# Down projection of a two-layer fp32 trunk: seven of sixteen weight pairs by seven products, some low parts of weights formed by a DMA that adds, relu and square of those pairs on ScalarE

## The chip, the core and the metric

The kernel runs on one core of one Trainium2 chip. A core has TensorE (matmuls), VectorE, ScalarE and GpSimd (elementwise work), SyncE (which here only issues DMAs), and 16 DMA engines that move data between HBM and the on-chip memory SBUF. Matmuls write to the banks of PSUM. The metric is the time of the whole kernel on the device, in microseconds (us).

## What is computed

The reference is a decoder trunk of two layers on 256 tokens of width 1024: RMSNorm, attention and a residual, then RMSNorm, an MLP and a residual; a final RMSNorm at the end. The change touches the MLP alone, above all its second matrix, which is 4096 x 1024 in float32:

```python
def squared_relu_mlp(x, w_up, w_down):
    return jnp.square(jax.nn.relu(x @ w_up)) @ w_down
```

## The kernel before

**Two parts for each number.** A float32 matmul is made of three matmuls in the faster format fp32r. Each factor is split in two parts: "hi" is the value rounded to fp32r (ScalarE, a copy, L153), "lo" is the value less hi (VectorE, a subtraction, L154). Then hi x hi, hi x lo and lo x hi are added up in PSUM. `split` (L148) does it for 128 x 1024 weights at a time.

**Weights.** They come from HBM in chunks of 1 MB (`row_chunk`, `col_chunk`, `pair_chunk`) into one of three buffers of the pool `wraw` (tiles "raw"); SyncE issues the load as soon as the buffer's last reader is done. The parts go to the pools `whi` and `wlo`, seven buffers of 128 x 1024 each, which come free in turn as TensorE is done with them. `plan` (L198 to L211) lists all chunks; `chunk(i)` emits the code for two chunks ahead of use. The order of TensorE's instructions is that of the code. On VectorE, ScalarE, GpSimd and SyncE a scheduler lays it out when the program is built, and each engine then works through its list in order.

**Stage of w_up.** 16 chunks of 256 columns; TensorE sums two times 128 columns in PSUM (`up_steps`), and `put_up` (L755) takes them out: ScalarE copies one half (L765), VectorE adds the other (L766), and VectorE forms relu and square in one instruction (L768). Both results are split again into hi and lo for the next stage (L778, L779).

**Stage of w_down.** The 32 row blocks of 128 rows go in 16 pairs of two. `MIXED` (L28) lists 12 pairs, and the kind says how a pair is multiplied. "W" (`whole_pair`, `whole_part`): both blocks, both halves of the 256 tokens and both halves of the 1024 columns, 8 products of 128 x 128 by 128 x 512, each of three matmuls, 24 in all. "S" (`seven_pair`, `seven_part`): the 2 x 2 x 2 blocks are multiplied by the Winograd form of Strassen's scheme, with 7 products and so 21 matmuls. It needs sums of weight blocks, made on VectorE in place in the raw buffer (L184, L185, L188, L189), three splits of 128 x 1024 in place of two (the plain left half, the sums in the right half, and the left half as it was changed in place), one of 128 x 512 (L191, L192), and on the other side sums of the hidden values (L774 to L776, split into `diffs` at L781 and L782). Before, pairs 2, 4, 6, 8 and 10 were S. Row blocks 24 to 31 (`REST`) follow in four chunks of four blocks by 512 columns, and before them `put_products` (L874) adds up what the seven products left in four PSUM banks.

**Pools that matter beside these.** `tmp` (six buffers "t") holds the small tiles of `put_up` and of the S pairs; `act` (two buffers "x2") holds the normed input of w_up, the differences, and later the next layer's inputs or final_norm.

Of the kernel before, what the change touches and what calls it, by code (L numbers as in the profile page):

```python
# [11 lines left out]
ALU = mybir.AluOpType  # L12
# [55 lines left out]
def yoco_kernel(  # L68
# [30 lines left out]
    def f(ap):  # L99
        return ap.bitcast(F32)  # L100
# [98 lines left out]
    for layer in range(2):  # L199
        wq, wk, wv = ([moba_w_qkv[0][:, i * D:(i + 1) * D] for i in range(3)] if layer == 0 else  # L200
                      [fox_w_q[0], w_kv[:, 0:D], w_kv[:, D:2 * D]])
        if layer:
            plan += [(row_chunk, wv, k0, 0) for k0 in (0, CK)]
        for g in range(4):
            plan += [(col_chunk, wq, g * S), (col_chunk, wk, g * S)]
            if g == 1:
                plan += [(row_chunk, wv, k0, NB) for k0 in (0, CK)]
        plan += [(row_chunk, w_o[layer], k0, nb * NB) for nb in range(2) for k0 in (0, CK)]
        plan += [(col_chunk, w_up[layer], i * S) for i in range(FF // S)]
        plan += [({"W": whole_pair, "S": seven_pair}[kind], w_down[layer], p) for kind, p in MIXED]  # L210
        plan += [(row_chunk, w_down[layer], k0, nb * NB) for nb in range(2) for k0 in REST[::CK]]  # L211
    first_of = [0]

    def load(n):
# [431 lines left out]

    fill = []
    for layer in range(2):
        r = inv_rms(sums)
        rbs = []  # L650
        qk = big.tile([P, 2, KC, S], F32, name="b0")
# [96 lines left out]


        hid.clear()  # L750
        both_ = act.tile([P, 2, 16, P], F32R, name="x2")
        diffs = both_[:, 0], both_[:, 1]


        def put_up(fc, accs):  # L755
            if not hid:
                hid.extend([big.tile([P, 16, S], F32R, name=name) for name in names]
                           for names in (("b0", "b1"), ("b2", "b3")))
            hh, hl = hid[0][fc // 16], hid[1][fc // 16]
            n = len(accs)  # L760
            a = slice(fc % 16, fc % 16 + n)
            u = tmp.tile([P, 2, S], F32, name="t")
            for j, ps in enumerate(accs):
                cp = tmp.tile([P, S], F32, name="t")
                nc.scalar.copy(cp, ps[:, S:2 * S])  # L765
                nc.vector.tensor_add(u[:, j], ps[:, 0:S], cp)  # L766
            sq = tmp.tile([P, 2, S], F32, name="t")
            nc.vector.scalar_tensor_tensor(sq[:, 0:n], u[:, 0:n], 0.0, u[:, 0:n], op0=ALU.max, op1=ALU.mult)  # L768
            if fc // 2 in SEVEN:


                us = tmp.tile([P, 3, P], F32, name="t")
                a11, a12, a21 = sq[:, 0, 0:P], sq[:, 1, 0:P], sq[:, 0, P:S]
                nc.vector.tensor_sub(us[:, 0:2], sq[:, 0].rearrange("p (t s) -> p t s", s=P), sq[:, :, P:S])  # L774
                nc.vector.tensor_sub(us[:, 2], us[:, 1], a11)
                nc.vector.tensor_add(a21, us[:, 2], a12)  # L776
                at = slice(3 * SEVEN.index(fc // 2), 3 * SEVEN.index(fc // 2) + 3)
            nc.scalar.copy(hh[:, a], sq[:, 0:n])  # L778
            nc.vector.tensor_sub(hl[:, a], sq[:, 0:n], f(hh[:, a]))  # L779
            if fc // 2 in SEVEN:  # L780
                nc.scalar.copy(diffs[0][:, at], us)  # L781
                nc.vector.tensor_sub(diffs[1][:, at], us, f(diffs[0][:, at]))  # L782

        def up_steps(i, c):
            accs = []
# [73 lines left out]


        def seven_part(c, p, i):
            n = SEVEN.index(p)
            place, at, factor = (
                (prod["w"], hidden_part(2 * p, 0), "b11"), (acc[0, 0], hidden_part(2 * p + 1, 0), "b21"),
                (acc[0, 1], hidden_part(2 * p, 1), "b22"), (prod["u3"], 0, "t3"), (prod["u1"], 1, "t1"),
                (prod["u2"], 2, "t2"), (acc[1, 0], hidden_part(2 * p + 1, 1), "t4"))[i]
            if isinstance(at, int):
                at = diffs[0][:, 3 * n + at], diffs[1][:, 3 * n + at]
            (hi, lo), j = c[factor]
            own = place in prod.values()  # L870
            mm_parts(place, at, (hi[:, j], lo[:, j]), own and n == 0, own and n == len(SEVEN) - 1)


        def put_products():  # L874
# [13 lines left out]
            add(1, 1, z)  # L888

        edge = []  # L890
        for i, (kind, p) in zip(take(len(MIXED)), MIXED):
            if kind == "W":
                fill += [((), 1300, lambda i=i, p=p, j=j: whole_part(chunk(i), p, j), None) for j in range(2)]
            else:
                fill += [((), 650, lambda i=i, p=p, n=n: seven_part(chunk(i), p, n), None) for n in range(7)]
        fill.append(((), 0, put_products, None))
        for nb in range(2 - layer):
            cs = take(len(REST) // CK)

            def rest_part(nb, cs, k, half):  # L900
                mm_rows(acc[half, nb], *hidden(k), half, chunk(cs[(k - REST[0]) // CK]), k % CK, False, k == REST[-1])
                if (k, half) == (REST[-1], 1):
                    down_done(nb, [acc[t, nb] for t in range(2)])

            fill += [((), 648, lambda nb=nb, cs=cs, k=k, half=half: rest_part(nb, cs, k, half),
                      pe.after((("h", nb, 0), 850), (("h", nb, 1), 1500)) if (k, half) == (REST[-1], 1) else None)
                     for k in REST for half in range(2)]
# [5 lines left out]
    cs = take(len(REST) // CK)  # L913
    ps = [acc[half, 1] for half in range(2)]

    def last_chunk(k):
        return chunk(cs[(k - REST[0]) // CK])

    def last_part(half, k, n):
        mm_rows(ps[half], *hidden(k), half, last_chunk(k), k % CK, False, k == n - 1)  # L920


    LAST = 2
# [25 lines left out]
    for k in REST[:-2 * CK]:  # L949
        for half in range(2):  # L950
            last_part(half, k, FF // P)
    for k in range(FF // P - 2 * CK, FF // P):
        last_part(0, k, FF // P)
    add_last(0, ps[0], 0, NB)
    finish(0, mean(square(0, 0, NB), part[:, 0:1]))
    for k in range(FF // P - 2 * CK, FF // P - LAST):
        last_part(1, k, FF // P - LAST)
    add_last(1, ps[1], 0, NB)
    sums_of = part[:, 1:2]
    for n0, (pool, name) in ((0, (psa, "acc")), (S, (psa, "acc"))):  # L960
        p = pool.tile([P, S], F32, name=name)
        for k in range(FF // P - LAST, FF // P):
            xh, xl, kx = hidden(k)
            t = slice(P, 2 * P)
            hi, lo = last_chunk(k)[k % CK // 2]
            for st, mv in ((xh, hi), (xh, lo), (xl, hi)):
                nc.tensor.matmul(p, st[:, kx, t], mv[:, k % 2, n0:n0 + S], start=k == FF // P - LAST and mv is hi and st is xh,
                                 stop=k == FF // P - 1 and st is xl)
# [32 lines left out]
```

## Time and profile before

| | us |
|---|---|
| median of three runs | 592.63 (592.06 to 592.75) |
| profiled execution, its own time | 592.5 |
| its span | 590.8 |
| TensorE busy (matmuls) | 581.8, 98% |
| VectorE busy | 462.7, 78% |
| ScalarE busy | 341.8, 58% |
| GpSimd busy | 10.1, 2% |
| weights read from HBM | 102.32 MB, 175 GB/s over the span |

The stage of w_down of layer 0 begins at 210.07 us of the span. The profile names engines PE (TensorE), PEld (its weight loads), DVE (VectorE), ACT (ScalarE), POOL (GpSimd) and SP (SyncE). A row of a timeline has the start, the length, the engine, the line, the operation and the tiles (out <- in); in brackets stands how long the engine sat idle just before, and whose result ended that. A row with "x5" merges five in succession. SyncE's rows are issues of DMAs, not their duration.

### The profile page before, as it was taken

What the parts mean: (1) busy time and instruction counts of PE and PEld (TensorE: products, weight loads), DVE (VectorE), ACT (ScalarE), POOL (GpSimd) and SP (SyncE); (2) the same over time, 40 slices, a digit from 0 to 9 for tenths busy, and PEclk for the clock granted to TensorE, in tenths of its full rate; (3) what the DMA queues carried; (4) which work ended last, traced back from release to release, by engine and by line L of the source; (5) the groups of instructions that cost most, each with busy time, mean ns of one, the idle gap of its engine ahead of it and who ended that gap; (6) DMA issues with size and microseconds to landing.
All of it is one profiled execution on the core that took longest, in us unless ns stands there. A gap on an engine that the chain in (4) does not pass through costs nothing.

```text
span 590.8 us, 8877 instructions
## 1 busy us (share of the span) xinstructions
PE 581.8 (98%) x3388; PEld 501.0 (85%) x3388; DVE 462.7 (78%) x834; ACT 341.8 (58%) x597; POOL 10.1 (2%) x39
## 2 busy tenths in 40 slices
PE   8999999999999999999999999999999999999995
PEld 6998997788888888888889989978888888888884
DVE  5887476489998878888788976767899896999853
ACT  6766566466566654654674665667565564564622
POOL 3000000000000000000000000000000000000000
PEclk9999999999999999999999999999999999999998
DMA  8984442458566517478446444433766664447601
GB/s 270 315 276 143 143 143 73 143 160 267 161 196 213 164 56 263 161 265 282 156 156 209 146 142 143 141 115 103 205 201 179 200 210 148 174 152 277 216 0 72
DMA packets 70890, 103.94 MB, mean 176 GB/s; under 512 B 1800, under 2 KB 51504, under 8 KB 70848
## 3 DMA queue, kind: packets, MB, share of 16 engines
q1 hardware_dynamic: 70336, 102.26, 53.5%
q0 software_dynamic: 208, 0.59, 0.3%
q8 instruction: 26, 0.43, 0.3%
q10 hardware_dynamic: 304, 0.53, 0.2%
q14 instruction: 16, 0.13, 0.1%
HBM read 102.32 MB, written 1.05 MB: 175 GB/s over the span
## 4 chain that ended last, share of the span: by engine, by line
PE 97%; DMA 1%; SPq 0%; DVE 0%; ACT 0%; issue 0%; POOLq 0%; DVEq 0%; ACTq 0%
PE acc L250 19%; PE acc L254 9%; PE sc L260 5%; PE sc L261 5%; PE sc L262 5%; PE acc L241 5%; PE acc L242 5%; PE acc L243 5%; PE acc L233 5%; PE acc L235 4%; PE acc L234 4%; PE sc L234 2%; PE sc L235 2%; PE sc L233 2%; PE sc L396 2%; PE pv L408 1%
## 5 line engine op out<-in xcount | busy, mean ns | idle before, releaser
L154 DVE TENSOR_TENSOR lo<-raw,hi 128x1024 fp32r<-128x1024 f32 x198 | 238.5, 1220 | 46.4 <-ACT hi L153 45.3
L153 ACT ACTIVATE hi<-raw 128x1024 fp32r<-128x1024 f32 x198 | 205.8, 1058 | 111.2 <-DVE raw L189 35.7
L250 PE MATMUL acc<-x,hi 128*128 128x512 f32 x480 | 164.6, 396 | 0.0
L254 PE MATMUL acc<-x,lo 128*128 128x256 f32 x480 | 124.2, 279 | 0.0
L250 PEld LDWEIGHTS acc<-x,hi 128*128 128x128 f32 x480 | 86.0, 188 | 16.3
L254 PEld LDWEIGHTS acc<-x,lo 128*128 128x128 f32 x480 | 90.5, 188 | 5.3
L241 PE MATMUL acc<-x,hi 128*128 128x256 f32 x256 | 74.1, 289 | 0.0
L242 PE MATMUL acc<-x,hi 128*128 128x256 f32 x256 | 72.4, 283 | 0.0
L243 PE MATMUL acc<-x,lo 128*128 128x256 f32 x256 | 72.4, 283 | 0.0
L765 ACT COPY t<-acc 128x256 f32<-128x256 f32 x60 | 22.3, 372 | 65.8 <-PE acc L250 63.2
L260 PE MATMUL sc<-hi,b 128*128 128x512 f32 x142 | 55.3, 389 | 0.0
L262 PE MATMUL sc<-hi,b 128*128 128x512 f32 x142 | 55.2, 389 | 0.0
L261 PE MATMUL sc<-lo,b 128*128 128x512 f32 x142 | 55.2, 389 | 0.0
L241 PEld LDWEIGHTS acc<-x,hi 128*128 128x128 f32 x256 | 49.0, 191 | 1.8 <-issue 1.7
L242 PEld LDWEIGHTS acc<-x,hi 128*128 128x128 f32 x256 | 49.0, 191 | 0.1
L243 PEld LDWEIGHTS acc<-x,lo 128*128 128x128 f32 x256 | 49.0, 191 | 0.0
L766 DVE TENSOR_TENSOR t<-acc,t 128x256 f32<-128x256 f32 x60 | 25.1, 421 | 14.1 <-ACT t L765 13.0
L381 ACT ACTIVATE t<-t,nm 128x128 f32<-128x128 f32 x64 | 28.3, 443 | 7.6 <-DVE nm L374 7.6
L262 PEld LDWEIGHTS sc<-hi,b 128*128 128x128 f32 x142 | 26.6, 188 | 5.6
L261 PEld LDWEIGHTS sc<-lo,b 128*128 128x128 f32 x142 | 26.7, 188 | 5.5
L260 PEld LDWEIGHTS sc<-hi,b 128*128 128x128 f32 x142 | 26.7, 188 | 5.5
L233 PE MATMUL acc<-hi,b 128*128 128x512 f32 x64 | 26.6, 415 | 0.0
(184 smaller groups left out, 886.8 us busy)
## 6 DMA issues: line engine op xcount, KB each, us to landing
raw<-in_w_up_dram SPq DMA_DIRECT2D x32, 1024.0 KB, 5.7
raw<-in_w_down_dram SPq DMA_DIRECT2D x32, 1024.0 KB, 4.8
raw<-in_moba_w_qkv_dram SPq DMA_DIRECT2D x10, 1024.0 KB, 5.3
raw<-in_w_o_dram SPq DMA_DIRECT2D x8, 1024.0 KB, 4.9
raw<-in_w_kv_dram SPq DMA_DIRECT2D x8, 1024.0 KB, 5.4
raw<-in_fox_w_q_dram SPq DMA_DIRECT2D x4, 1024.0 KB, 5.0
raw<-in_moba_w_qkv_dram SPq DMA_DIRECT2D x3, 512.0 KB, 7.6
h<-in_x_dram SPq DMA_DIRECT2D x2, 256.0 KB
```

The lines of the kernel that those rows point to most:

```text
L153: nc.scalar.activation(hi[:, i:i + n], raw[:, i:i + n], AF.Copy)
L154: nc.vector.tensor_sub(lo[:, i:i + n], raw[:, i:i + n], f(hi[:, i:i + n]))
L233: nc.tensor.matmul(ps, xh[:, kx, t], hi[:, kw % 2], start=start, stop=False)
L234: nc.tensor.matmul(ps, xh[:, kx, t], lo[:, kw % 2], start=False, stop=False)
L241: nc.tensor.matmul(ps, hi[:, k], xh[:, k], start=k == 0, stop=False)
L242: nc.tensor.matmul(ps, hi[:, k], xl[:, k], start=False, stop=False)
L243: nc.tensor.matmul(ps, lo[:, k], xh[:, k], start=False, stop=k == KC - 1)
L250: nc.tensor.matmul(ps, hi[:, k], x2[:, k].rearrange("p t s -> p (t s)"), start=k == 0, stop=k == KC - 1)
L254: nc.tensor.matmul(ps[:, 0:S], lo[:, k], xh[:, k], start=False, stop=False)
L260: nc.tensor.matmul(ps, x[0], w[0], start=start, stop=False)
L261: nc.tensor.matmul(ps, x[0], w[1], start=False, stop=False)
L262: nc.tensor.matmul(ps, x[1], w[0], start=False, stop=stop)
```

## The change

- `MIXED` now has a list for each layer (both are the same): W for pairs 0, 1, 3, 6 and 9, S for pairs 2, 4, 5, 7, 8, 14 and 15. What is left (`REST`) are row blocks 20 to 27.
- `split` takes a `source`. Where it has one, ScalarE writes the negated rounded weights into lo (L156 of the new file) and the rounded ones into hi (L157), and a DMA issued from GpSimd adds the weights from HBM onto lo (L158): lo = w - hi, without VectorE. It is used from pair 3 on: for the second block of each W pair, and for the plain left half of each S pair. That makes nine such DMAs of 512 KB in a layer.
- `put_up` forms relu and square of S pairs in two steps on ScalarE (L793, L794) in place of one on VectorE.
- The differences of the first five S pairs are split as before; those of pairs 14 and 15 go to a second tile "x2", in the buffer that held w_up's input.

```diff
+BY_DMA = (1,)
+FIRST = 2
+MIXED = [[("W", 0), ("W", 1), ("S", 2), ("W", 3), ("S", 4), ("S", 5), ("W", 6), ("S", 7), ("S", 8), ("W", 9), ("S", 14), ("S", 15)],
...
-    def split(raw, pieces=1):
+    def split(raw, pieces=1, source=None):
         hi = whi.tile([P] + list(raw.shape[1:]), F32R, name="hi")
         lo = wlo.tile([P] + list(raw.shape[1:]), F32R, name="lo")
+        if source is not None:
+            nc.scalar.activation(lo, raw, AF.Copy, scale=-1.0)
+            nc.scalar.activation(hi, raw, AF.Copy)
+            nc.gpsimd.dma_start(lo, source, accum_op=ALU.add)
+            return hi, lo
...
     def whole_pair(w, p):
         raw = pair_chunk(w, p)
-        return [split(raw[:, k].rearrange("p (n c) -> p n c", c=NB)) for k in range(2)]
+        rows = [w[(2 * p + k) * P:(2 * p + k + 1) * P].rearrange("p (n c) -> p n c", c=NB) for k in range(2)]
+        return [split(raw[:, k].rearrange("p (n c) -> p n c", c=NB), source=rows[k] if k in BY_DMA and p > FIRST else None)
+                for k in range(2)]
...
-        plain = split(left)
+        plain = split(left, source=w[2 * p * P:(2 * p + 2) * P, 0:NB].rearrange("(c p) n -> p c n", p=P) if p > FIRST else None)
...
+        def split_diffs():
+            while len(diffs) < len(kept):
+                n = len(diffs)
+                if n % 5 == 0:
+                    room.append(act.tile([P, 2, 16, P], F32R, name="x2"))
+                dh, dl = (room[-1][:, i, n % 5 * 3:n % 5 * 3 + 3] for i in range(2))
+                nc.scalar.copy(dh, kept[n])
+                nc.vector.tensor_sub(dl, kept[n], f(dh))
+                diffs.append((dh, dl))
...
-            nc.vector.scalar_tensor_tensor(sq[:, 0:n], u[:, 0:n], 0.0, u[:, 0:n], op0=ALU.max, op1=ALU.mult)
-            if fc // 2 in SEVEN:
+            if fc // 2 in seven:
+                nc.scalar.activation(u[:, 0:n], u[:, 0:n], AF.Relu)
+                nc.scalar.activation(sq[:, 0:n], u[:, 0:n], AF.Square)
+            else:
+                nc.vector.scalar_tensor_tensor(sq[:, 0:n], u[:, 0:n], 0.0, u[:, 0:n], op0=ALU.max, op1=ALU.mult)
```

**The lists of the engines.** In the new file `split` has its lines at L162 (hi) and L163 (lo), and the additions of an S pair are L195, L196, L199 and L200 (L184, L185, L188 and L189 before), its 128 x 512 split L202 and L203. The numbers behind tile names tell buffers of one name apart. The first place is ScalarE's list early in the stage of w_down of layer 0. Before, from the changed left half of S2 on (raw_2389 is pair 2, raw_2436 pair 3, raw_2470 pair 4), it reads:

```order
L153 ACTIVATE hi_2408<-raw_2389 128x1024
L153 ACTIVATE hi_2438<-raw_2436 128x1024
L153 ACTIVATE hi_2442<-raw_2436 128x1024
L153 ACTIVATE hi_2475<-raw_2470 128x1024
L153 ACTIVATE hi_2483<-raw_2470 128x1024
L153 ACTIVATE hi_2489<-raw_2470 128x1024
```

In the new program the same stretch (raw_2409 is pair 2, raw_2456 pair 3, raw_2491 pair 4, raw_2536 pair 5) reads:

```order
L162 ACTIVATE hi_2428<-raw_2409 128x1024
L162 ACTIVATE hi_2458<-raw_2456 128x1024
L157 ACTIVATE hi_2462<-raw_2456 128x1024
L157 ACTIVATE hi_2496<-raw_2491 128x1024
L162 ACTIVATE hi_2505<-raw_2491 128x1024
L156 ACTIVATE lo_2463<-raw_2456 128x1024
L156 ACTIVATE lo_2497<-raw_2491 128x1024
L202 ACTIVATE t_2546<-t_2538 128x512
L162 ACTIVATE hi_2511<-raw_2491 128x1024
L157 ACTIVATE hi_2541<-raw_2536 128x1024
```

The negated copies of pair 3 (lo_2463) and pair 4 (lo_2497), on which the adding DMAs wait, stand sixth and seventh, behind the rounded copies.

The second place is VectorE's list where the last S pairs begin. Before (raw_2626 is pair 8, raw_2670 pair 9, raw_2704 pair 10) it reads:

```order
L184 TENSOR_TENSOR t_2706<-raw_2704 128x512
L154 TENSOR_TENSOR lo_2646<-raw_2626,hi_2645 128x1024
L185 TENSOR_TENSOR raw_2704<-raw_2704 128x512
L154 TENSOR_TENSOR lo_2673<-raw_2670,hi_2672 128x1024
L154 TENSOR_TENSOR lo_2677<-raw_2670,hi_2676 128x1024
L192 TENSOR_TENSOR t_2714<-t_2706,t_2713 128x512
L154 TENSOR_TENSOR lo_2710<-raw_2704,hi_2709 128x1024
```

In the new program (raw_2661 is pair 8, raw_2741 pair 14, raw_2786 pair 15) it reads:

```order
L163 TENSOR_TENSOR lo_2682<-raw_2661,hi_2681 128x1024
L195 TENSOR_TENSOR t_2743<-raw_2741 128x512
L163 TENSOR_TENSOR lo_2712<-raw_2709,hi_2711 128x1024
L196 TENSOR_TENSOR raw_2741<-raw_2741 128x512
L203 TENSOR_TENSOR t_2752<-t_2743,t_2751 128x512
L195 TENSOR_TENSOR t_2788<-raw_2786 128x512
L199 TENSOR_TENSOR raw_2741<-raw_2741 128x512
L196 TENSOR_TENSOR raw_2786<-raw_2786 128x512
L163 TENSOR_TENSOR lo_2756<-raw_2741,hi_2755 128x1024
L200 TENSOR_TENSOR raw_2741<-raw_2741 128x512
```

Pair 15 takes the raw buffer of pair 8, which lo_2682 is the last to read, and its first instruction (t_2788) now stands ahead of the rest of pair 14.

The third place is ScalarE's list just after that, where L200 above has to be done before hi_2761:

```order
L162 ACTIVATE hi_2761<-raw_2741 128x1024
L157 ACTIVATE hi_2791<-raw_2786 128x1024
L162 ACTIVATE hi_2800<-raw_2786 128x1024
L156 ACTIVATE lo_2792<-raw_2786 128x1024
L162 ACTIVATE hi_2806<-raw_2786 128x1024
```

There is no such row before: lo_2710, the plain low part of the last S pair, was VectorE's (above), and now lo_2792, the negated copy, is fourth here, with its DMA behind it.

## Rows read from the trace of the kernel before

**Rows 1.** The page's first part: busy us (share) x instructions of each engine.

```profile
PE 581.8 (98%) x3388; PEld 501.0 (85%) x3388; DVE 462.7 (78%) x834; ACT 341.8 (58%) x597; POOL 10.1 (2%) x39
```

**Rows 2.** The page's fourth part: the chain that ended last, by engine.

```profile
PE 97%; DMA 1%; SPq 0%; DVE 0%; ACT 0%; issue 0%; POOLq 0%; DVEq 0%; ACTq 0%
```

**Rows 3.** Windows: length; busy PE, PEld, DVE, ACT, POOL; clock, DMA share, GB/s.

```profile
215.00:235.00 20.00, 20.00 (x90) 16.56 (x89) 17.59 (x21) 10.98 (x12) 0.00 (x0) 1.00 0.49 171
235.00:255.00 20.00, 20.00 (x90) 16.54 (x89) 17.59 (x21) 10.98 (x12) 0.00 (x0) 1.00 0.55 204
```

**Rows 4.** Timeline of TensorE: first matmul of w_down, first of the remaining chunks.

```profile
210.07 0.40 PE L260 MATMUL sc<-hi,b 128*128 128x512 f32 x1
...
271.97 0.39 PE L233 MATMUL sc<-hi,b 128*128 128x512 f32 x1
```

**Rows 5.** The chain that ended last in order of time: two chunks of w_up.

```profile
198.81 0.47 PE acc L250 x2
204.41 0.47 PE acc L250 x2
```

**Rows 6.** Timeline of VectorE: end of w_up and start of w_down.

```profile
185.48 0.42 DVE L766 TENSOR_TENSOR t<-acc,t 128x256 f32<-128x256 f32 x1
185.83 0.28 DVE L775 TENSOR_TENSOR t<-t 128x128 f32<-128x128 f32 x1
186.14 0.29 DVE L776 TENSOR_TENSOR t<-t 128x128 f32<-128x128 f32 x1
186.45 1.22 DVE L154 TENSOR_TENSOR lo<-raw,hi 128x1024 fp32r<-128x1024 f32 x1
187.59 0.55 DVE L782 TENSOR_TENSOR x<-t,x 128x384 fp32r<-128x384 f32 x1
188.06 0.68 DVE L779 TENSOR_TENSOR b<-t,b 128x512 fp32r<-128x512 f32 x1
188.66 0.42 DVE L766 TENSOR_TENSOR t<-acc,t 128x256 f32<-128x256 f32 x1
...
210.73 0.42 DVE L766 TENSOR_TENSOR t<-acc,t 128x256 f32<-128x256 f32 x1 [2.37 <-ACT t L765]
...
217.27 0.68 DVE L189 TENSOR_TENSOR raw<-raw 128x512 f32<-128x512 f32 x1
...
219.09 5.77 DVE L154 TENSOR_TENSOR lo<-raw,hi 128x1024 fp32r<-128x1024 f32 x5 [0.53 <-ACT hi L153]
```

**Rows 7.** Timeline of ScalarE in the same stretch.

```profile
212.58 0.63 ACT L191 ACTIVATE t<-t 128x512 fp32r<-128x512 f32 x1
...
217.99 4.86 ACT L153 ACTIVATE hi<-raw 128x1024 fp32r<-128x1024 f32 x5 [2.31 <-DVE raw L189]
```

**Rows 8.** Timeline of SyncE: issues of w_down's loads.

```profile
222.61 0.37 SPq L172 DMA_DIRECT2D raw<-in_w_down_dram  x1
229.89 3.24 SPq L172 DMA_DIRECT2D raw<-in_w_down_dram  x2
240.17 2.64 SPq L172 DMA_DIRECT2D raw<-in_w_down_dram  x2
```

**Rows 9.** Timeline of VectorE: S pairs that wait for a load; a last pair's splits.

```profile
228.03 0.69 DVE L184 TENSOR_TENSOR t<-raw 128x512 f32<-128x512 f32 x1 [1.85 <-DMA raw<-in_w_down_dram]
237.59 0.69 DVE L184 TENSOR_TENSOR t<-raw 128x512 f32<-128x512 f32 x1 [0.65 <-DMA raw<-in_w_down_dram]
248.27 0.69 DVE L184 TENSOR_TENSOR t<-raw 128x512 f32<-128x512 f32 x1 [1.66 <-DMA raw<-in_w_down_dram]
253.49 2.35 DVE L154 TENSOR_TENSOR lo<-raw,hi 128x1024 fp32r<-128x1024 f32 x2
```

**Rows 10.** The page's sixth part: DMA issues, KB each, median us to landing.

```profile
raw<-in_w_down_dram SPq DMA_DIRECT2D x32, 1024.0 KB, 4.8
x<-in_final_norm_dram POOLq DMA_DIRECT2D x1, 512.0 KB, 4.0
```

**Rows 11.** GpSimd's instruction for that load; ns min/median/max, start.

```profile
L826 POOL DMA_DIRECT2D x<-in_final_norm_dram x1: 588/588/588, 500.8 to 500.8; - x1
```

More of the change, by code (lines that the diff above doesn't have):

```diff
@@ L209, in yoco_kernel @@
         plan += [(col_chunk, w_up[layer], i * S) for i in range(FF // S)]
-        plan += [({"W": whole_pair, "S": seven_pair}[kind], w_down[layer], p) for kind, p in MIXED]
-        plan += [(row_chunk, w_down[layer], k0, nb * NB) for nb in range(2) for k0 in REST[::CK]]
+        plan += [({"W": whole_pair, "S": seven_pair}[kind], w_down[layer], p) for kind, p in MIXED[layer]]
+        plan += [(row_chunk, w_down[layer], k0, nb * NB) for nb in range(2) for k0 in REST[layer][::CK]]
     first_of = [0]
@@ L648, in yoco_kernel @@
     for layer in range(2):
+        mixed, seven, rest = MIXED[layer], SEVEN[layer], REST[layer]
         r = inv_rms(sums)
@@ L750, in yoco_kernel @@
         hid.clear()
[L751 to L752 removed]
+        diffs, kept = [], []
+        def split_diffs():
[7 more added lines that the diff above has]
+                diffs.append((dh, dl))
+        room = []
         def put_up(fc, accs):
@@ L776, in put_up @@
                 nc.vector.tensor_add(a21, us[:, 2], a12)
-                at = slice(3 * SEVEN.index(fc // 2), 3 * SEVEN.index(fc // 2) + 3)
             nc.scalar.copy(hh[:, a], sq[:, 0:n])
             nc.vector.tensor_sub(hl[:, a], sq[:, 0:n], f(hh[:, a]))
-            if fc // 2 in SEVEN:
-                nc.scalar.copy(diffs[0][:, at], us)
-                nc.vector.tensor_sub(diffs[1][:, at], us, f(diffs[0][:, at]))
+            if fc // 2 in seven:
+                kept.append(us)
+                if len(kept) <= 5 or fc + 2 == FF // P:
+                    split_diffs()
         def up_steps(i, c):
@@ L861, in seven_part @@
         def seven_part(c, p, i):
-            n = SEVEN.index(p)
+            n = seven.index(p)
             place, at, factor = (
@@ L867, in seven_part @@
             if isinstance(at, int):
-                at = diffs[0][:, 3 * n + at], diffs[1][:, 3 * n + at]
+                at = tuple(d[:, at] for d in diffs[n])
             (hi, lo), j = c[factor]
             own = place in prod.values()
-            mm_parts(place, at, (hi[:, j], lo[:, j]), own and n == 0, own and n == len(SEVEN) - 1)
+            mm_parts(place, at, (hi[:, j], lo[:, j]), own and n == 0, own and n == len(seven) - 1)
         def put_products():
@@ L890, in yoco_kernel @@
         edge = []
-        for i, (kind, p) in zip(take(len(MIXED)), MIXED):
+        for i, (kind, p) in zip(take(len(mixed)), mixed):
             if kind == "W":
@@ L897, in yoco_kernel @@
         for nb in range(2 - layer):
-            cs = take(len(REST) // CK)
+            cs = take(len(rest) // CK)
             def rest_part(nb, cs, k, half):
-                mm_rows(acc[half, nb], *hidden(k), half, chunk(cs[(k - REST[0]) // CK]), k % CK, False, k == REST[-1])
-                if (k, half) == (REST[-1], 1):
+                mm_rows(acc[half, nb], *hidden(k), half, chunk(cs[rest.index(k) // CK]), k % CK, False, k == rest[-1])
+                if (k, half) == (rest[-1], 1):
                     down_done(nb, [acc[t, nb] for t in range(2)])
             fill += [((), 648, lambda nb=nb, cs=cs, k=k, half=half: rest_part(nb, cs, k, half),
-                      pe.after((("h", nb, 0), 850), (("h", nb, 1), 1500)) if (k, half) == (REST[-1], 1) else None)
-                     for k in REST for half in range(2)]
+                      pe.after((("h", nb, 0), 850), (("h", nb, 1), 1500)) if (k, half) == (rest[-1], 1) else None)
+                     for k in rest for half in range(2)]
             pe.run([edge, fill], fill)
@@ L910, in yoco_kernel, with last_part @@
                 edge += norm_steps(nb, [(gs[:, 2], *xkv[:2]), (gs[:, 1], *xa[:2])])
-    cs = take(len(REST) // CK)
+    cs = take(len(rest) // CK)
     ps = [acc[half, 1] for half in range(2)]
     def last_chunk(k):
-        return chunk(cs[(k - REST[0]) // CK])
-    def last_part(half, k, n):
-        mm_rows(ps[half], *hidden(k), half, last_chunk(k), k % CK, False, k == n - 1)
+        return chunk(cs[rest.index(k) // CK])
+    def last_part(half, k, last):
+        mm_rows(ps[half], *hidden(k), half, last_chunk(k), k % CK, False, k == last)
     LAST = 2
@@ L947, in finish @@
         nc.scalar.dma_start(outr[:, half, NB:D], y[:, NB:D])
-    for k in REST[:-2 * CK]:
+    for k in rest[:-2 * CK]:
         for half in range(2):
-            last_part(half, k, FF // P)
-    for k in range(FF // P - 2 * CK, FF // P):
-        last_part(0, k, FF // P)
+            last_part(half, k, rest[-1])
+    for k in rest[-2 * CK:]:
+        last_part(0, k, rest[-1])
     add_last(0, ps[0], 0, NB)
     finish(0, mean(square(0, 0, NB), part[:, 0:1]))
-    for k in range(FF // P - 2 * CK, FF // P - LAST):
-        last_part(1, k, FF // P - LAST)
+    for k in rest[-2 * CK:-LAST]:
+        last_part(1, k, rest[-1 - LAST])
     add_last(1, ps[1], 0, NB)
@@ L961, in yoco_kernel @@
         p = pool.tile([P, S], F32, name=name)
-        for k in range(FF // P - LAST, FF // P):
+        for k in rest[-LAST:]:
             xh, xl, kx = hidden(k)
@@ L966, in yoco_kernel @@
             for st, mv in ((xh, hi), (xh, lo), (xl, hi)):
-                nc.tensor.matmul(p, st[:, kx, t], mv[:, k % 2, n0:n0 + S], start=k == FF // P - LAST and mv is hi and st is xh,
-                                 stop=k == FF // P - 1 and st is xl)
+                nc.tensor.matmul(p, st[:, kx, t], mv[:, k % 2, n0:n0 + S], start=k == rest[-LAST] and mv is hi and st is xh,
+                                 stop=k == rest[-1] and st is xl)
         add_last(1, p, n0, n0 + S)
```

7 lines of the change are left out of this document (4 added, 3 removed).

## The prediction

> **What bounds the kernel now.** I read the page's first part, then the chain that ended last, then the stage of w_down itself. TensorE is busy 581.8 of 590.8 us [rows 1], and the chain that ended last is TensorE for 97% of the span [rows 2]. Within the stage of w_down it is busy for every microsecond of both windows, at full clock, while VectorE has 17.59 of 20 us and ScalarE 10.98 of 20 [rows 3]. So a matmul taken out is time won, as long as nobody makes TensorE wait for weights, and VectorE has little left to give. From the first matmul of the stage at 210.07 us to the first of the remaining chunks at 271.97 lie 273 matmuls, seven whole pairs of 24 and five pairs of seven products with 21 [rows 4]. That is 61.90 / 273 = 0.2267 us each: 5.44 us for a whole pair (W below), 4.76 for a pair by seven products (S below). Times below are counted from the first of these matmuls, t = 0 at 210.07; S8 is pair 8 by seven products, and its "more" is the third split, that of the left half after it was changed in place.
>
> **What is removed.** Two more pairs of each layer go from 24 matmuls to 21: 4 x 3 = 12 matmuls, 12 x 0.2267 = 2.72 us, 1.36 a layer, all on the bounding engine. If nothing waits, the time is 592.5 - 2.7 = 589.8 us. Everything else in the change lies on engines beside TensorE, and the question is whether the weights still come in time.
>
> **What is moved to other engines.** VectorE has 7 splits fewer a layer in this stage (nine go to the DMAs, two more S pairs bring two) and ten additions more: 10 x 0.69 - 7 x 1.22 = -1.6 us, and about as much again in the up stage. ScalarE gains eleven activations of 128x1024 and sixteen of 128x512 a layer: 11 x 1.06 + 16 x 0.62 = 21.6 us (durations below). It has the room by share. In the up stage these fit: a chunk takes TensorE 5.6 us [rows 5], and two splits with the work of one S pair stay under that on both engines, so I price the up stage at nothing; cover gone, it would show as TensorE waiting for a PSUM bank at L789. The shares hide what matters: in the stage of w_down each engine works its list in order, and the weights run through three raw buffers. So I add up one chain.
>
> **Pitches for the chain.** On VectorE one instruction follows the other after 1.14 us for 128x1024 (186.45 to 187.59), 0.60 for 128x512 (188.06 to 188.66), 0.47 for 128x384, 0.35 for 128x256 and 0.31 for 128x128; the last of a row is done 1.22 us after its start for 128x1024 and 0.69 for 128x512 [rows 6]. On ScalarE five copies of 128x1024 take 4.86 us, so 0.95 pitch and 1.06 for the last; 128x512 takes 0.62 [rows 7]. From engine to engine I count 0.05 (217.95 to 217.99) [rows 6, 7]. A raw buffer is asked for again by SyncE when its last split ends, and VectorE goes on with the new data after 228.03 - 222.61 = 5.42, 237.59 - 232.76 = 4.83 and 248.27 - 242.44 = 5.83 us (the second of two issues starts at the row's start plus its length less 0.37) [rows 8, 9]. I call this reload R and take 5.4, the mean of the three.
>
> **The chain, step by step.** Start: the last up column reaches VectorE at 0.66 [rows 6]. In the order after, that pair (15) is an S pair, so VectorE waits for relu and square on ScalarE, 1.1 + 2 x 0.62 = 2.35, and then has thirteen instructions up to L200 of S2 (lines of the new file): seven of 128x512 (4.2), one of 128x1024 (1.14), one of 384 (0.47), one of 256 (0.35), two of 128 (0.62), then L200 itself from 9.2 to 9.9. The copy "hi" of S2's more (ScalarE) ends at 11.0, its low part (VectorE) at 12.25. In the kernel before the same low part ended at 219.09 + 1.22 - 210.07 = 10.24 [rows 6].
> (1) This frees the raw buffer for S5. Its data come at 12.25 + R; VectorE does L195, L199, L196, L200 (1.8 + 0.69), ScalarE the copy (1.06), VectorE the low part (1.22): 4.9 us, and S4's buffer is free.
> (2) That buffer takes S7. After R, L195 and the last low part of S5: 1.8 us.
> (3) S5's buffer takes S8. After R, five of 128x512, three of 128x1024 and L200 on VectorE (6.4 + 0.69), then copy and low part of S8's more: 9.5 us.
> (4) S8's buffer takes S15. After R, L195, L199, L196, one split and L200 (3.6), then on ScalarE three copies and at last the negated copy of S15's plain part (3 x 0.95 + 1.06): 7.6 us.
> (5) Only now can the adding DMA of S15 start; it needs L us.
> TensorE wants this low part with the second matmul of S15, after 246 + 1 matmuls: 247 x 0.2267 = 56.0. So it comes late by 12.25 + 4.9 + 1.8 + 9.5 + 7.6 + 4R + L - 56.0 = 4R + L - 20 us. In the kernel before, the low part of the last S pair was done at 253.49 + 1.22 - 210.07 = 44.6 [rows 9], and TensorE wanted it after 229 matmuls, at 51.9: 7.3 us early. Two S pairs in a row, twice, and a DMA at the chain's end use that up and more.
>
> **What the adding DMA costs (L).** No DMA that adds is in the trace. From below: a plain DMA of the same 512 KB from GpSimd's queue took 4.0 us to land [rows 10]. From above: twice that, 8.0, if what lies in the buffer is fetched in a pass of its own. I take 5.0, since it has to read 512 KB of weights and 512 KB of the buffer, and a 1024 KB load takes 4.8 [rows 10]; it is nearest to that row. GpSimd's own 0.59 us for the issue [rows 11] is a part of it.
> The Trainium skill ("DMA: Bandwidth & Descriptors", section "Anatomy of one DMA") gives about 2.0 us plus bytes / 436e3 for a DMA from GpSimd: 3.2 us for 512 KB, an estimate by that page, under the 4.0 of the row, and it says nothing of adding. By it the delay would be 4.8 us a layer and the time 599.4.
>
> **The sum.** With R = 5.4 and L = 5.0 the delay is 21.6 + 5.0 - 20 = 6.6 us a layer. It falls in four pieces, whose total is the 6.6: the low part of W3's second half is the sixth copy after S2's more on ScalarE (9.95 + 5 x 0.95 + 1.06 = 15.75), lands at 20.75 and is wanted at 82 x 0.2267 = 18.6: 2.1 us. S5, S8 and S15 wait for theirs by the same working, some 1, 0.5 and 3 us. Less the 1.36 won: 5.24 a layer, and the second layer's lists stand in the same order, so 10.5 us in all. The profiled execution takes 592.5 us (span 590.8 and 1.7 around it), 0.1 under the median 592.63: 592.5 + 10.5 = 603.0 us. The layer-1 load of final_norm now stands in GpSimd's queue ahead of S15's adding DMA; it waits for S8's products (before 50 with the delays so far), so it costs its issue at most, 0.6 us, hidden by S15's wait for ScalarE.
>
> **Ends.** Low: R = 4.8 (the shortest of the three), L = 4.0: 3.2 us late, 592.5 + 2 x (3.2 - 1.36) = 596.2. High: R = 6.8 (the longest, 5.83, and once more the 1.0 by which a load beside another is longer than one alone) and L = 8.0: 15.2 late, 592.5 + 2 x 13.8 = 620.
>
> **Rivals.** (a) The DMA engines become the bound. Nine adding DMAs in some 42 us bring 4.7 MB of weights and as much of the buffer: 225 GB/s on top of some 190. The stretches show 171 GB/s at a share of 0.49 and 204 at 0.55 [rows 3], so full engines give about 350 to 370. Loads and adds would then wait for each other, R and L both at their high ends or over: about 620 us. For it: the sum over the limit. Against it: whether the buffer's own bytes count so is not seen here. The Trainium skill (same page, "Issuing engines are not separate DMA queues") says that DMAs of all queues run on the same 16 engines; the 5.83 beside 4.83 agrees. (b) It works as drawn: no wait, 589.8. The place is the negated copy and adding DMA of S15; it is decided at 4R + L under 20, for R = 4.8 at L under 0.8. Against it: the plain DMA's 4.0. For it: the chain holds 36 us of my pitches, and 5% less of these is 1.8 us. (c) The waits just eat the gain, 4R + L about 21.4: R = 4.8 and L = 2.2, 592.5 us. (d) The change doesn't shed VectorE's work as it says, since ScalarE's list then holds it up at L199 (which waits for both copies of the plain part): that is within the chain and would lengthen steps 3 and 4, towards the high end.
>
> **How the numbers follow.** Forecast (one chain of reloads, 596 to 615) 0.71; (a) with the long end of (d) 0.18; (c) 0.05; (b) 0.06. Predicted: 603.0 us. The range 595.5 to 620 leaves out (b), (c) and about half of (a). Faster by over 0.2% (under 591.4): 0.06; within 0.2%, about what can be told from no change: 0.05; slower: 0.89.
>
> **What would show it.** TensorE no longer busy throughout the stage: waits at L271 to L273 for a DMA into "lo", four a layer, the longest at S15, 5 to 8 us a layer. From the stage's first matmul to the first of the remaining chunks 267 x 0.2267 = 60.5 us plus the delay, so 66 to 69 in place of 61.9. Landing times of the adding DMA give L, those of w_down's loads R (the forecast is wrong if L is under 3 or R under 4.8). ScalarE's busy time some 40 us higher, VectorE's a few lower, the up stage as long as before. If the waits are there but at the loads into "raw" and the DMA share is near 1, it was (a); if TensorE doesn't wait, the chain is wrong.

## The result, and the profile after

The changed kernel takes 620.0 us (median of four runs, 616.8 to 621.6) against 592.5 us: a ratio of 1.0452, with an interval of 1.0431 to 1.0474. It is 27.5 us slower; the forecast was 10.5 us slower, and 620 was the far end of its range. The profiled execution of the changed kernel took 618.5 us, with a span of 616.8.

The page's first part (busy us, share, instructions) and its fourth (the chain that ended last, by engine) answer to [rows 1, 2]:

```profile
PE 587.5 (95%) x3376; PEld 502.0 (81%) x3376; DVE 457.6 (74%) x842; ACT 383.1 (62%) x655; POOL 29.7 (5%) x57
```

```profile
PE 74%; DMA 12%; DVE 8%; ACT 3%; issue 2%; SPq 0%; POOLq 0%; DVEq 0%; ACTq 0%
```

TensorE has 12 matmuls fewer, as drawn, but the chain that was 97% TensorE is now 12% DMA and 8% VectorE. The issues on the page's sixth part answer to [rows 10] (KB each, median us to landing):

```profile
raw<-in_w_down_dram SPq DMA_DIRECT2D x32, 1024.0 KB, 6.1
lo<-in_w_down_dram POOLq DMA_DIRECT2D x18, 512.0 KB, 8.9
```

The loads of w_down took 4.8 us before. The same two stretches of the w_down stage as [rows 3], in windows (length; busy PE, PEld, DVE, ACT, POOL; clock, DMA share, GB/s):

```profile
215.00:235.00 20.00, 14.81 (x63) 11.94 (x62) 15.33 (x20) 12.68 (x16) 3.35 (x3) 0.90 0.60 154
235.00:255.00 20.00, 18.87 (x76) 14.79 (x74) 12.02 (x15) 12.35 (x14) 3.25 (x3) 0.93 0.93 256
```

TensorE, without a gap before, makes 63 and 76 matmuls where it made 90; the DMA share goes from 0.55 to 0.93 in the second stretch, and even VectorE is less busy. The time is lost in this stage alone: from its first matmul (209.7 us) to the first of the remaining chunks (285.0) it takes 75.3 us in the first layer and 74.9 in the second, against 61.9 before [rows 4], in either layer. That is 13.4 and 13.0 us more, 26.5 together, and the span grew by 26.0.

The chain that ended last in the first layer's stage, in order of time (start us, us, what):

```profile
220.42 1.24 DVE lo L163
221.68 4.81 DMA raw<-in_w_down_dram
226.50 0.69 DVE t L195
...
230.19 1.24 DVE lo L163
231.44 7.96 DMA raw<-in_w_down_dram
239.42 0.69 DVE t L195
240.11 1.15 DVE lo L163
241.28 5.78 DMA raw<-in_w_down_dram
...
255.49 1.24 DVE lo L163
256.74 9.93 DMA raw<-in_w_down_dram
...
273.45 0.96 ACT lo L156
274.40 0.29 issue
274.69 5.58 DMA lo<-in_w_down_dram
280.32 0.50 PE acc L272
```

This is the chain of the prediction, link by link: four reloads into raw buffers, the negated copy of S15 on ScalarE, its adding DMA, and TensorE's second matmul of S15. TensorE starts it at 280.32, t = 70.6, where it wanted 56.0: 14.6 us late.

### The profile page after: what moved, and what is told of

Read it like the earlier page. It is cut to its first block, busy times and chain, and to the rows that moved or that the text cites. A ratio compares the mean times of both kernels' runs of the same rounds, so it can differ in the third digit from the quotient of the medians.

```text
span 616.8 us, 9006 instructions
## 1 busy us (share of the span) xinstructions
PE 587.5 (95%) x3376; PEld 502.0 (81%) x3376; DVE 457.6 (74%) x842; ACT 383.1 (62%) x655; POOL 29.7 (5%) x57
## 4 chain that ended last, share of the span: by engine, by line
PE 74%; DMA 12%; DVE 8%; ACT 3%; issue 2%; SPq 0%; POOLq 0%; DVEq 0%; ACTq 0%
PE acc L261 18%; PE acc L265 9%; DMA raw<-in_w_down_dram 9%; PE acc L252 5%; PE acc L254 5%; PE acc L253 5%; PE acc L244 4%; PE acc L246 4%; PE acc L245 4%; DVE lo L163 3%; PE sc L246 2%; PE sc L244 2%; PE sc L245 2%; DMA lo<-in_w_down_dram 2%; PE sc L407 2%
## 5 line engine op out<-in xcount | busy, mean ns | idle before, releaser
L163 DVE TENSOR_TENSOR lo<-raw,hi 128x1024 fp32r<-128x1024 f32 x184 | 223.2, 1221 | 57.7 <-ACT hi L162 55.9
L162 ACT ACTIVATE hi<-raw 128x1024 fp32r<-128x1024 f32 x184 | 192.2, 1058 | 92.8 <-PE acc L253 27.8
L272 PE MATMUL sc<-lo,b 128*128 128x512 f32 x122 | 50.3, 412 | 10.9 <-DMA lo<-in_w_down_dram 10.8
L273 PE MATMUL sc<-hi,b 128*128 128x512 f32 x122 | 49.5, 406 | 0.0
L271 PE MATMUL sc<-hi,b 128*128 128x512 f32 x122 | 49.3, 404 | 0.0
L272 PEld LDWEIGHTS sc<-lo,b 128*128 128x128 f32 x122 | 24.1, 198 | 17.7 <-DMA lo<-in_w_down_dram 12.6
L158 POOL DMA_DIRECT2D lo<-in_w_down_dram x18 | 19.6, 1090 | 276.6 <-ACT lo L156 158.4
L195 DVE TENSOR_TENSOR t<-raw 128x512 f32<-128x512 f32 x14 | 9.7, 690 | 27.1 <-DMA raw<-in_w_down_dram 24.9
L273 PEld LDWEIGHTS sc<-hi,b 128*128 128x128 f32 x122 | 24.3, 199 | 5.1
```

The lines of the kernel that those rows point to most:

```text
L271: nc.tensor.matmul(ps, x[0], w[0], start=start, stop=False)
L272: nc.tensor.matmul(ps, x[0], w[1], start=False, stop=False)
L273: nc.tensor.matmul(ps, x[1], w[0], start=False, stop=stop)
```

## The experiments

Each edit is to the changed kernel. Ratios are to the kernel before, run on the same chip.

### No adding DMA, and the old order with it

Two suspects go with the seven pairs: the adding DMAs, and pairs by seven products that stand in a row. One run has the new order without the DMAs, one the old order (five such pairs, each between whole pairs) with nine adding DMAs a layer.

```
-BY_DMA = (1,)
-FIRST = 2
+BY_DMA = ()
+FIRST = 99
```

> The changed kernel with its seven pairs, relu and square on ScalarE, but no adding DMA: VectorE forms every low part, the nine 512 KB adds of a layer are gone. Theory (loads of w_down queue behind the adds, so the chain of four reloads is 7.1 us a piece in place of 5.4, and the last add is on top): reloads land in about 5 us again, TensorE waits 0 to 4 us a layer for VectorE alone, 590 to 598 us, nearest 595. Rival (S pairs in a row are too much for VectorE and ScalarE, DMA or not, and nine splits more make it worse): 605 us or over.

Measured 596.5 us, ratio 1.0069 (1.0053 to 1.0085): the main theory. Of the distance of 30.2 us between 620.0 and the 589.8 of the count, 23.5 go with the adding DMAs (less what VectorE's nine splits more cost) and 6.7 are left without them. The trace shows some 4 us of these as waits of TensorE for ScalarE and VectorE; how they divide between the new order and VectorE's longer list is not shown.

```
-... ("S", 4), ("S", 5), ("W", 6), ("S", 7), ("S", 8), ("W", 9), ("S", 14), ("S", 15)
+... ("S", 4), ("W", 5), ("S", 6), ("W", 7), ("S", 8), ("W", 9), ("S", 10), ("W", 11)
```

> The five S pairs of the kernel before, in its order (every S pair between two W pairs), with the nine adding DMAs a layer and relu and square on ScalarE. Theory: the adds alone make loads and low parts late; reloads land in 6 us or more, the 7 us of slack at the last S pair are used up, 597 to 606 us, nearest 601. Rival (the pairs in a row cause it): no waits of TensorE, 592 to 593 us.

Measured 604.3 us, 1.0203 (1.0187 to 1.0218). The adds cost 11.8 us even where no two such pairs are neighbours; the rival is out. TensorE waits 2.5 us for the add of W3's second half and 0.6 for that of S4's plain left half. The second one, issued 0.9 us behind the first, is the late link in the chain of the first layer:

```profile
223.94 12.12 DMA lo<-in_w_down_dram
```

### What of the add it is: the bytes, or the adding

The same DMA as a plain copy, and an add that covers one eighth of its columns:

```
-            nc.gpsimd.dma_start(lo, source, accum_op=ALU.add)
+            nc.gpsimd.dma_start(lo, source)
```

> The changed kernel with the nine DMAs of a layer as plain copies in place of adds: same issue, same 512 KB from HBM, same place in the lists, but the buffer's own bytes are not read (the low parts are then wrong, so the output is not the reference's). If reading the buffer and adding costs the DMA engines a pass of its own: landing 4 to 6 us in place of 8.9, loads nearer to 5.4, delay about 9 us a layer, 604 to 611 us. Rival (the adds cost what any 512 KB cost): 618 to 622 us.

Measured 601.3 us, 1.0149 (1.0128 to 1.0171), under the expected band and far from the rival.

```
-            nc.gpsimd.dma_start(lo, source, accum_op=ALU.add)
+            nc.gpsimd.dma_start(lo[:, 0:1, 0:P], source[:, 0:1, 0:P], accum_op=ALU.add)
```

> The changed kernel with each adding DMA cut to an eighth (128 of 1024 columns a partition, 64 KB; the rest of the low part stays unfinished, so the output is not the reference's). The wait for an add and its fixed time stay, its traffic is nearly gone. Theory (traffic): reloads 5.4 us, landing 3 to 4.5, delay 4R + L - 20 = 5 to 6 us a layer, 599 to 603 us. Rival (an add is slow whatever its size): landing 6 us and over, 606 us and over.

Measured 597.7 us, 1.0092 (1.0075 to 1.0109), a little under the expected band: the path over ScalarE, GpSimd's queue and a DMA costs about 1 us beside no add at all, as long as few bytes go over it. That is net of the splits that VectorE is spared: TensorE still waits 2.2 us in the first layer and 2.1 in the second for W3's low part.

So bytes matter, and adding them matters more. The page's third part has the time of the queues (packets, MB, share of the 16 engines' span); the row of GpSimd's queue for the changed kernel, for the plain copy and without those DMAs, one fence each:

```profile
q0 software_dynamic: 4336, 10.03, 8.5%
```

```profile
q0 software_dynamic: 4336, 10.03, 4.9%
```

```profile
q0 software_dynamic: 208, 0.59, 0.3%
```

The same packets and bytes take (8.5 - 0.3)% of 616.8 us = 50.6 us of all engines as adds and (4.9 - 0.3)% of 601.3 = 27.7 us as copies: 2.8 and 1.5 us for one of 512 KB, 1.83 times as much. With copies the first layer's four reloads were 4.75, 4.78, 4.80 and 5.50 us, at or under the R of the prediction; with adds they were 4.81, 7.96, 5.78 and 9.93. In the second layer the copies give back only a part: 4.71, 4.82, 7.44 and 6.04, against 4.81, 7.75, 5.67 and 7.99.

### A fourth raw buffer

If the chain of reload after reload sets the time, a fourth raw buffer must give it back. Room comes from the buffers of the parts, so that a control is needed:

```
-    whi = ctx.enter_context(tc.tile_pool(name="whi", bufs=7))
-    wlo = ctx.enter_context(tc.tile_pool(name="wlo", bufs=7))
+    whi = ctx.enter_context(tc.tile_pool(name="whi", bufs=6))
+    wlo = ctx.enter_context(tc.tile_pool(name="wlo", bufs=6))
```

> The changed kernel with six instead of seven buffers each for the high and the low parts; a control for the next one. Theory: the chain of reloads goes through the three raw buffers and not through these, so 617 to 624 us, nearest 620. Rival (the low parts' buffers are a link of the chain, since a negated copy needs a free one before its add can start): 626 us or more.

Measured 615.0 us, 1.0390 (1.0376 to 1.0403): 5 us less than the changed kernel, and less than expected. Why fewer buffers help is not settled; its chain has reloads of 4.90, 7.37, 5.47 and 6.89 us and a last add of 8.15, 32.8 us in place of 34.1.

```
-    wraw = ctx.enter_context(tc.tile_pool(name="wraw", bufs=3))
+    wraw = ctx.enter_context(tc.tile_pool(name="wraw", bufs=4))
```

> The same six buffers of each, and a fourth raw buffer in the room that comes free, so that each reload may start one pair earlier. Theory (the lateness of 14.6 us a layer is a chain of reload after reload, each waiting for the last work on its buffer): most of it goes; what stays is the engines' own time, about 25 us of adds and 52 us of loads a layer against some 65 us with what is loaded ahead, so 4 to 6 us late a layer: 598 to 609 us, nearest 604. Rival (the DMA engines are full and set the time whatever the buffers): within 1% of the control, 614 us or more.

Measured 615.1 us, 1.0381 (1.0368 to 1.0395): no change against the control. The theory of the chain of buffers fell. VectorE hardly waits for loads any more (6.4 us in all at L195, against 24.9 in the changed kernel), and the wait has moved into the adds, which now take 10.1 us at the median:

```profile
raw<-in_w_down_dram SPq DMA_DIRECT2D x32, 1024.0 KB, 5.1
lo<-in_w_down_dram POOLq DMA_DIRECT2D x18, 512.0 KB, 10.1
```

With the fourth buffer kept, the add becomes a copy:

> Four raw buffers and six of each part, as in the run before with those, but the DMA of the low part copies in place of adding (the same bytes on the same queue from the same places; these low parts are then wrong). Theory (with four raw buffers it is the DMA engines that are full: 25 us of adds beside 52 us of loads a layer; as copies they take 14 us): 594 to 602 us, nearest 598, at least 13 us under the same kernel with adds. Rival (the time lies in the path from the load over ScalarE, GpSimd and the second DMA to TensorE, whatever the engines' share): 608 us or more.

Measured 600.7 us, 1.0138 (1.0114 to 1.0163), 14.4 us under the same kernel with adds: the theory of full engines. One window over most of the first layer's stage (columns as above), for four raw buffers with adds, four with copies, the changed kernel, no adds, and the kernel before:

```profile
228.00:288.00 60.00, 51.15 (x211) 40.57 (x210) 41.00 (x49) 37.41 (x39) 8.54 (x8) 0.94 0.98 273
```

```profile
228.00:288.00 60.00, 56.52 (x252) 46.48 (x252) 48.69 (x56) 41.73 (x46) 4.78 (x8) 1.00 0.89 305
```

```profile
228.00:288.00 60.00, 48.69 (x201) 38.49 (x200) 39.23 (x47) 35.76 (x39) 7.67 (x7) 0.94 0.94 259
```

```profile
228.00:288.00 60.00, 57.03 (x250) 46.09 (x249) 55.37 (x65) 34.67 (x40) 0.00 (x0) 1.00 0.60 212
```

```profile
228.00:288.00 60.00, 60.00 (x270) 49.80 (x269) 50.44 (x57) 33.31 (x43) 0.00 (x0) 1.00 0.65 228
```

With four buffers and adds the DMA engines are busy 0.98 of these 60 us, move 273 GB/s, and TensorE makes 211 matmuls. With copies they move 305 GB/s at 0.89, and it makes 252. So engines that are full set the time; with three raw buffers it shows in the chain of reloads, with four in the adds. Much of it then goes with a single add. The first layer's stage with four buffers and adds is 12.6 us longer than the 60.5 of the count. TensorE waits 8.9 us in it for low parts, 5.5 of them for W3's second half, and comes back from that wait at half its clock (below) for a dozen matmuls:

```profile
234.56 0.80 PE L272 MATMUL sc<-lo,b 128*128 128x512 f32 x1 [5.50 <-DMA lo<-in_w_down_dram]
```

### Fewer adds

Seven adds a layer (without W3's and S4's), then two (only the second blocks of W6 and W9):

```
-FIRST = 2
+FIRST = 4
```

> The changed kernel without the two first adding DMAs of a layer (whole pair 3 and seven-product pair 4 on VectorE): seven adds a layer from pair 5 on. Theory (the DMA engines are full from the first add to the last, so each add taken away gives back its 2.8 us of the engines, less VectorE's 1.2 us for the low part): 620 less 4 x 2.8 to 4 x 1.6, 608.7 to 613.6 us, nearest 611. Rival one (the chain of reloads with unchanged waits for its other links: only the second load gets 2.5 us shorter and VectorE longer by as much): 616 us or more. Rival two (the first wait of TensorE and its half clock cost time of their own, 5.2 us and more a layer): 607 us or less.

Measured 606.4 us, 1.0234 (1.0217 to 1.0251), under the band of the theory and within that of rival two. The four adds gave back 13.6 us. Both things that I had set against each other are seen: in the first layer the reloads for S7 and S8 are back at 4.79 and 4.75 us, and TensorE's first long wait with its half clock (below) is gone. In the second layer a later wait, of 2.7 us, still ends at half clock. How much is whose, this run doesn't tell.

```
-FIRST = 2
+FIRST = 3
-        plain = split(left, source=w[...] if p > FIRST else None)
+        plain = split(left, source=None)
```

> The changed kernel with two adding DMAs a layer instead of nine (second block of pairs 6 and 9 only); the other seven low parts on VectorE. By the count 589.8 us if nothing waits. Theory (an add takes 50.6 / 18 = 2.8 us of all DMA engines, and these only stretch the stage where they are full, which two adds do not do; what stays is VectorE, relieved of 2 x 1.23 us a layer against 596.5 us without any add): 592 to 596 us, nearest 594, and the w_down load back at 4.7 to 5.0 us. Rival (each add costs its share of the 23.5 us between no add and eighteen, 1.3 us): 596.5 + 4 x 1.3 = 601.7 us, 599 us or more.

Measured 604.3 us, 1.0207 (1.0192 to 1.0222): the theory missed, since two adds are worse than none by 7.8 us, and the rival has the number but not the reason. It is one add a layer, that of W6. TensorE's timeline there, and GpSimd's (start us, us, instruction, in brackets the idle time before it and what ended that):

```profile
243.39 0.39 PE L271 MATMUL sc<-hi,b 128*128 128x512 f32 x1
248.19 0.79 PE L272 MATMUL sc<-lo,b 128*128 128x512 f32 x1 [4.42 <-DMA lo<-in_w_down_dram]
248.78 0.63 PE L273 MATMUL sc<-hi,b 128*128 128x512 f32 x1
249.21 0.63 PE L271 MATMUL sc<-hi,b 128*128 128x512 f32 x1
```

```profile
240.20 0.91 POOL L158 DMA_DIRECT2D lo<-in_w_down_dram  x1 [114.25 <-ACT lo L156]
```

TensorE wanted the low part at 243.8. Without adds TensorE does not wait there, so VectorE has it in time; here ScalarE has its negated copy ready at 240.2, 3.6 us ahead, and the add takes 7.95 us more. It runs beside loads, and for as long as it takes (240.2 to 248.1) the DMA share is 0.99:

```profile
240.20:248.10 7.90, 3.57 (x16) 2.63 (x14) 7.90 (x11) 4.19 (x5) 0.91 (x1) 0.94 0.99 284
```

TensorE waits 4.4 us and then runs 13 matmuls 0.43 us apart instead of 0.23, another 2.6 us. The second layer's wait is 5.0 us. With as much at half clock there, that is 9.5 + 5.2 = 14.7 us, about all that lies between 589.8 and 604.3. That the engines have room on the mean (a share of 0.70 from 228 to 288) does not make a single add cheap: it puts 8 us of its own between the negated copy and the matmul.

### Other parts alone, and other ways to help VectorE

The rest of the change alone (relu and square on ScalarE, diffs kept per pair), with the five pairs in the old order and no adds:

> The five seven-product pairs of the kernel before, in its old order, every low part on VectorE; of the change only relu and square of those five pairs on ScalarE and the diffs kept per pair are left. Theory (those steps lie beside TensorE's work in the up stage): no change, 591.9 to 593.3 us, nearest 592.5. Rival (the up stage pays for the longer hand-over between ScalarE and VectorE): 594 us or more, since one matmul of waiting for each of the ten pairs would already be 10 x 0.2267 = 2.3 us.

Measured 592.5 us, 1.0000 (0.9991 to 1.0009): free, as priced.

Six pairs instead of seven, no adds, pairs 2, 4, 6, 8, 10 and 15. (Its remaining rows of w_down meet hidden rows shifted by two blocks, so the output is another; the work is the same.)

> Six pairs by seven products (2, 4, 6, 8, 10 and 15, with a whole pair before each but the last), all low parts on VectorE, relu and square of the six on ScalarE, no adding DMA. Each layer has 6 matmuls fewer than the kernel before: 2 x 6 x 0.2267 = 2.7 us by the count, or half of it against five pairs with three matmuls fewer a pair. Theory (what costs time is the pairs in a row and the adding DMAs, and neither is here): 589.8 to 592.0 us, nearest 591.1. Rival (VectorE's list is already full with five pairs, so that a sixth pair waits for it): 593.5 us or more, with waits of TensorE for low parts of VectorE.

Measured 593.4 us, 1.0027 (1.0012 to 1.0042): in neither band, nearest to the rival's, but not for its reason. TensorE does not wait for any low part; in the first layer it waits at the stage's end, 0.57 and 0.99 us in front of the transposes of L320, for VectorE's L860. So VectorE is behind here too, at the end of its list, and the matmuls saved are lost again.

The five second blocks of whole pairs subtracted on GpSimd, idle otherwise, in place of the adds:

```
-FIRST = 2
+FIRST = -1
...
-            nc.scalar.activation(lo, raw, AF.Copy, scale=-1.0)
             nc.scalar.activation(hi, raw, AF.Copy)
-            nc.gpsimd.dma_start(lo, source, accum_op=ALU.add)
+            nc.gpsimd.tensor_sub(lo, raw, f(hi))
...
-        plain = split(left, source=w[...] if p > FIRST else None)
+        plain = split(left)
```

> The changed kernel with no adding DMA; the low part of the second block of each of the five whole pairs is subtracted on GpSimd, all others on VectorE. Theory (what is left without adds, 596.5 us against 589.8 by the count, is VectorE's list, and five low parts of 1.24 us a layer off it are enough): 590 to 594 us, nearest 592; it would be the first version with seven pairs that is not slower than the kernel before. Rival (GpSimd's subtraction is as late as the adding DMA, or slows VectorE's instructions beside it): 598 us or more. No row of any run has a subtraction of this size on GpSimd; from VectorE's 1.24 us up to the 8 us of the adding DMA is the bound.

Measured 601.9 us, 1.0153 (1.0133 to 1.0173): the rival. GpSimd's subtraction, and VectorE's timeline across it:

```profile
238.72 2.80 POOL L157 TENSOR_TENSOR lo<-raw,hi 128x1024 fp32r<-128x1024 f32 x1 [13.18 <-DVE lo L162]
```

```profile
237.44 1.22 DVE L162 TENSOR_TENSOR lo<-raw,hi 128x1024 fp32r<-128x1024 f32 x1
238.58 0.68 DVE L195 TENSOR_TENSOR raw<-raw 128x512 f32<-128x512 f32 x1
239.18 4.55 DVE L162 TENSOR_TENSOR lo<-raw,hi 128x1024 fp32r<-128x1024 f32 x2
```

Two subtractions of VectorE take 4.55 us beside it, where two take 1.14 + 1.22 = 2.36 [rows 6]: it loses 2.2 us for the 1.14 it was spared. TensorE then waits for low parts of VectorE, in the first layer 1.5 and 2.3 us. The Trainium skill ("SBUF — State Buffer", section "SBUF: two separate sides") says that VectorE instructions with two inputs in SBUF and GpSimd's share a port that one of them holds for its whole instruction; the 4.55 us of the trace agree with it.

None of the versions run is faster than the kernel before.

## Why the prediction was right and wrong

**Right: the sign, the place, the chain and its work.** VectorE's low part of S2's more ended at t = 12.0 (12.25 forecast). The work between the reloads took 4.92, 1.84, 9.59 and 7.64 us, where I had added up 4.9, 1.8, 9.5 and 7.6. ScalarE is 41.3 us busier (some 40 forecast), VectorE 5.1 less; the up stage is as long as before, and relu and square on ScalarE cost nothing.

**Wrong: the step "R = 5.4".** This is the term that was mis-sized. In the first layer the four reloads took 4.81 + 7.96 + 5.78 + 9.93 = 28.5 us, 7.1 each, where 4R was 21.6: 6.9 us of the 8.0 by which S15's low part came later than forecast (14.6 in place of 6.6). L was 5.6 for S15's add (5.0 forecast), and 8.9 at the median of all; the rest are hand-overs of 0.1 to 0.3 us. In the second layer the reloads took 26.2 us and the last add 5.8, so that S15's low part came 12.7 us late, and half clock after that wait cost 1.8 more. 14.6 + 12.7 + 1.8, less twice the 1.36 won, is 26.4; the span grew by 26.0. That the far end of the range was 620 is partly luck: it was added up from R = 6.8 and L = 8.0, and measured were 7.1 and 5.6.

**Why R was wrong.** I took R from a trace without adds, in whose stage the DMA engines were busy half of the time, and wrote in the same text, as a rival, that the adds would bring more than the engines can do. The two belong together: a load's time is not a property of the load. The runs show that rival (a) is the cause: the same bytes as copies give R back in the first layer and a part of it in the second (601.3 us), and with a fourth raw buffer, where VectorE hardly waits for loads, the time is that of its control (615.1 and 615.0) at a DMA share of 0.98. The price that I had lacked is the engines' time for an add, 2.8 us for 512 KB. The landing time at which I had looked (4.0 to 8.0) does not tell it.

**Half right: four waits a layer.** In the first layer TensorE waited 5.2 us for W3's low part, 0.4, 0.8 and 1.6 us for three adds between, and 3.3 for S15's, against 2.1, 1, 0.5 and 3 forecast; W3's was furthest off. I had priced none of them with what follows: after W3's wait the matmuls stand 0.43 us apart for some 4 us. In the first layer later waits swallow this, since the chain that ends last runs beside it. In the second layer some nine matmuls at half clock follow S15's wait, about 1.8 us, and there nothing hides them.

**The other rivals.** (b) and (c) came nowhere near. (d) did not happen: with ScalarE's longer list, steps 3 and 4 took what I had added up.

## What to carry to other kernels

A duration read from a trace holds at that trace's load: where a change brings traffic, first add up the time of the DMA engines (bytes by what a byte of that kind takes) over the stage, and only where that leaves room use the landing times of before. A DMA put between a load and the matmul that needs it wants its whole landing time as lead, and under load that was 8 to 10 us at the median here, where the VectorE instruction that it replaced takes 1.2. If another buffer moves a wait without changing the time, look for the resource that is full rather than for the next buffer.

## What the runs showed of the hardware that I had not expected

**An adding DMA takes the engines 1.83 times as long as a copy of the same bytes** (50.6 against 27.7 us for eighteen of 512 KB), and it lands in 8.9 us at the median against 6.3. In the run with two adds a layer it is much the same: (2.1 - 0.3)% of 604.0 us for four, 2.7 us each, landing in 8.1 at the median. GpSimd's instruction for it is longer too: 1178 ns at the median against 698 for the copy. The estimate of 3.2 us by the Trainium skill ("DMA: Bandwidth & Descriptors", section "Anatomy of one DMA") is under every landing of 512 KB seen here, the plain ones included (4.0 [rows 10], and 4.3 to 9.5).

**TensorE comes back from a wait of some 5 us at half its clock.** TensorE's timeline of the changed kernel at W3's wait in the first layer:

```profile
228.03 0.39 PE L271 MATMUL sc<-hi,b 128*128 128x512 f32 x1
233.61 0.79 PE L272 MATMUL sc<-lo,b 128*128 128x512 f32 x1 [5.19 <-DMA lo<-in_w_down_dram]
234.20 0.63 PE L273 MATMUL sc<-hi,b 128*128 128x512 f32 x1
234.63 0.63 PE L271 MATMUL sc<-hi,b 128*128 128x512 f32 x1
```

And the windows around it:

```profile
224.00:228.00 4.00, 4.00 (x19) 3.34 (x18) 2.72 (x4) 2.71 (x4) 2.17 (x2) 1.00 0.93 294
...
234.00:236.00 2.00, 2.00 (x6) 1.52 (x6) 0.63 (x1) 1.06 (x1) 0.47 (x1) 0.50 1.10 267
```

(A share counts a packet where it starts, so a short window can show more than 1.) The granted clock is 1.00 (2.4 GHz) before the wait and 0.50 (1.2 GHz) after it, and a matmul follows the other after 0.43 us in place of 0.23. So a wait of 5 us cost 7 to 8 where nothing hid it, as in the run with two adds. All eight waits of 4.4 to 5.7 us in these runs ended like this. After the wait of 3.3 us for S15 in the first layer the clock stayed full. In the second layer it fell (to 0.50 from 583 to 586 us) after a shorter one:

```profile
581.76 0.50 PE L272 MATMUL acc<-lo,b 128*128 128x512 f32 x1 [2.25 <-DMA lo<-in_w_down_dram]
582.10 0.40 PE L273 MATMUL acc<-hi,b 128*128 128x512 f32 x1
582.34 0.40 PE L271 MATMUL sc<-hi,b 128*128 128x512 f32 x1
582.58 0.58 PE L272 MATMUL sc<-lo,b 128*128 128x512 f32 x1
582.95 0.63 PE L273 MATMUL sc<-hi,b 128*128 128x512 f32 x1
```

Neither the length nor the place of a wait tells. With copies in place of adds TensorE waited 3.0 us for W3's low part in each layer. The granted clock behind the first of these waits was 0.50 (232 to 234 us), behind the second 1.00 (526 to 529):

```profile
231.53 0.79 PE L272 MATMUL sc<-lo,b 128*128 128x512 f32 x1 [3.02 <-DMA lo<-in_w_down_dram]
...
525.68 0.50 PE L272 MATMUL sc<-lo,b 128*128 128x512 f32 x1 [3.04 <-DMA lo<-in_w_down_dram]
```

What does is open; no run was made for it.
